# Stick-breaking attention: score tiles grouped otherwise, PSUM copies and sigmoids issued at other steps

## The chip, the cores and the metric

The kernel runs on one core of a Trainium2 chip. The metric is the device time of one execution in microseconds. TensorE (PE) does matrix products and transposes, VectorE (DVE) and ScalarE (ACT) do elementwise work and copies, GpSimd (POOL) does small fills, and SyncE (SP) issues most DMA transfers. Each engine works through its own queue in program order; semaphores hold an instruction until what it reads is there and what it overwrites is no longer read. Matmuls write PSUM, from which ACT or DVE copy to SBUF.

## What is computed

One layer of a decoder with batch 1 and 512 new tokens behind 16 meta tokens, and 8 running sequences of 4 tokens with 256 cached ones. The width is 1024. Two SwiGLU blocks enclose a mixer in which gated linear attention and stick-breaking attention run side by side. The change lies in the stick-breaking attention of 16 heads of 64, computed per pair of heads:

```python
def block(args):
    qblk, qi = args
    z = jnp.einsum('bqhd,bkhd->bhqk', qblk, k).astype(jnp.float32) * scale + bias_f
    mask = k_idx[None, :] < qi[:, None]
    l = jnp.where(mask, jax.nn.log_sigmoid(-z), 0.0)
    r = lax.cumsum(l, axis=3, reverse=True) - l
    a = jnp.where(mask, jnp.exp(jax.nn.log_sigmoid(z) + r), 0.0)
    return jnp.einsum('bhqk,bkhd->bqhd', a.astype(v.dtype), v)
```

The kernel takes the product of 1 - sigmoid(z) itself as a scan over the keys, from the right. It also returns the new key and value rows, of prompt and sample.

## The kernel before

**Main work.** Everything is computed in fp32 split into a high and a low part, with three products for one. The attention stage (about 587 to 806 us) projects queries, keys and values for eight pairs of heads. Its main work is a generator, `attention()`, that yields after each step of six matmuls. A pair has 8 steps for its queries (`tile_steps`, L728, L729, L731) and, from pair 1 on, 14 for keys and values together (`seven_steps`, L1079 to L1081: a 2 x 2 block product in seven products, from weight blocks b1, t, b2 and t4 and their sums). So pairs begin 22 steps apart (`BEGIN`).

`seven_steps` works in four PSUM accumulators a, d, b and c, and passes partial sums on: two steps after its start ACT copies a to b (L1069), at four d to a room (L1059), at six b to c (L1069 again) and b to a room (L1059), and so on. Each weight block is cast to its high part on ACT (L1006) and its low part is taken on DVE (L172). `weights_at` puts these at steps counted from the pair's start.

**Extra work.** What a pair needs beyond its projections is queued while the main work of the next pair runs. With n = `BEGIN[pr + 1]`, the list `pieces` puts each function at a step n + d: `scores` (three tiles n = 0, 1, 2 of the score matrix of both heads; L1996 on PE, then for each head e two sigmoids on ACT, L2001 and L2002, and POOL's fills), `scan` (L2015 on DVE), `weigh` (a product on DVE through the helper at L172, and the copy L2025), `rows_v` and `rows_k` (the new rows turned on PE, copied by ACT at L2046 and L2035, stored by SP), `tails` (L2053 to L2055 on PE, four DVE instructions from L2059 on), `turned` (the weights turned, L2078 on PE and L2081 on ACT, at the steps of `TURN`) with `meta_turned` at its end (L2104, L2105). `summed` and `meta_summed` multiply by the values, in the next pair's time. Pairs 4 to 7 also handle cached keys of the sample: `sample_keys` at n+14 (sixteen transposes L2181, four ACT copies L2183) and `sample_products` at n+16. Functions at one step are issued in the order in which they were listed; `later(k, f)` issues f some k steps on. A run of PE instructions between two main matmuls is called a group below.

**What sets the order.** The block runs in a manual schedule: each engine's queue is the order in which the Python code issues. `ps()` hands out four rotating PSUM buffers for extra work (pool `pp`, bufs=4). SBUF rooms come from an `Arena`, whose `take` reads the next place from the table `PLACES`; a room may only be written again when the instructions that used the place before are done, and so the table decides some waits.

Of the kernel before, what the change touches and what calls it, by code (L numbers as in the profile page):

```python
# [9 lines left out]
F32 = mybir.dt.float32  # L10
# [6 lines left out]
P = 128  # L17
# [3 lines left out]
NS = 32  # L21
# [41 lines left out]
3830686a0c606670241c46678584404844762f1b62261a50381e3c8c2c301036184c28722e3e427a683a6b604a0c08864e0966677040157b620e
2556201e58541a2f24352268843c3826443e34508c6a3b420c32604a6e0a0b7686082a09464e7a6284823a330e382e483c0006688c66704c0402
3e2c182514126a160a6e6072404a3043360d1c2a483b3c4208522e402c44464d3330100c504e0e424801362a10001c333c4d443206503140423e
0c3b040e023c4e081c0030482a363e0e023b4e1144060d0400403c104a524c4842461c0230362a0c3e40003c4a3d0608110400023a38484f524e
# [70 lines left out]
def hybrid_step(  # L137
# [2653 lines left out]
```

## Time and profile before

| | |
|---|---|
| timed runs | 1493.84, 1492.57 and 1585.64 us; median 1493.84 |
| profiled execution | 1492.2 us, its span 1490.5 us, granted TensorE clock 0.999 |
| busy, share of the span | PE 1477.0 us (99%), DVE 1085.3 (73%), ACT 804.9 (54%), POOL 57.0 (4%) |
| chain that ended last | PE 94%, DVE 3%, ACT 1%, DMA 1% |
| matmul instructions | 11905 |

The chain of work that ended last is followed back from the last instruction. In a row of the timeline stand the start, the duration, engine, line, operation, what is written and read, and how many instructions are taken together; in brackets stand the idle time of the engine ahead of it and the instruction that ended it. Matmuls overlap: each reads about 0.29 us, while the next starts 0.13 us later, so distances between starts say more than durations. L172 is a helper for all elementwise operations of two tensors, so its rows are told apart by their shapes.

### The profile page before, as it was taken

What the parts mean: (1) busy time and instruction counts of PE and PEld (TensorE: products, weight loads), DVE (VectorE), ACT (ScalarE), POOL (GpSimd) and SP (SyncE); (2) the same over time, 40 slices, a digit from 0 to 9 for tenths busy, and PEclk for the clock granted to TensorE, in tenths of its full rate; (3) what the DMA queues carried; (4) which work ended last, traced back from release to release, by engine and by line L of the source; (5) the groups of instructions that cost most, each with busy time, mean ns of one, the idle gap of its engine ahead of it and who ended that gap; (6) DMA issues with size and microseconds to landing.
All of it is one profiled execution on the core that took longest, in us unless ns stands there. A gap on an engine that the chain in (4) does not pass through costs nothing.

```text
span 1490.5 us, 29845 instructions
## 1 busy us (share of the span) xinstructions
PE 1477.0 (99%) x11905; PEld 1421.8 (95%) x11905; DVE 1085.3 (73%) x1820; ACT 804.9 (54%) x1513; POOL 57.0 (4%) x175
## 2 busy tenths in 40 slices
PE   9999999999999999999999999999999999999998
PEld 8999999999999898888988999999999999999998
DVE  5888888855677866887776754676567898888544
ACT  7455445533555656766775543644564455455334
POOL 2000000000000011201100000000000000000000
PEclk9999999999999999999999999999999999999999
DMA  8133333224665686567676866434531333333252
GB/s 253 50 93 100 100 91 103 85 79 130 170 147 132 164 160 175 108 115 139 141 122 181 246 143 198 97 103 147 156 112 51 100 100 101 98 106 93 79 174 93
DMA packets 288540, 187.60 MB, mean 126 GB/s; under 512 B 10988, under 2 KB 266674, under 8 KB 288402
## 3 DMA queue, kind: packets, MB, share of 16 engines
q1 hardware_dynamic: 280706, 181.97, 45.5%
q0 software_dynamic: 7680, 3.74, 2.5%
q8 instruction: 93, 1.52, 0.4%
q14 instruction: 45, 0.37, 0.1%
q10 hardware_dynamic: 16, 0.00, 0.0%
HBM read 160.63 MB, written 25.03 MB: 125 GB/s over the span
## 4 chain that ended last, share of the span: by engine, by line
PE 94%; DVE 3%; ACT 1%; DMA 1%; issue 0%; SPq 0%; DVEq 0%; ACTq 0%
PE acc L1300 8%; PE acc L1301 8%; PE acc L1302 8%; PE acc L741 6%; PE acc L744 6%; PE acc L742 6%; PE acc L728 5%; PE acc L729 5%; PE acc L731 5%; PE acc L1079 4%; PE acc L1081 4%; PE acc L1080 4%; PE acc L1242 2%; PE acc L1239 2%; PE acc L1240 2%; PE ps L1996 1%
## 5 line engine op out<-in xcount | busy, mean ns | idle before, releaser
L172 DVE TENSOR_TENSOR room<-room,room 128x560 fp32r<-128x560 f32 (+12 forms) x470 | 294.0, 645 | 84.2 <-ACT room L1059 17.0
L172 DVE TENSOR_TENSOR lo<-raw,hi 128x1024 fp32r<-128x1024 f32 (+1 forms) x207 | 248.1, 1199 | 80.3 <-ACT hi L1006 42.5
L1300 PE MATMUL acc<-room,hi 128*128 128x280 f32 (+1 forms) x896 | 259.9, 290 | 0.0
L1301 PE MATMUL acc<-room,hi 128*128 128x280 f32 (+1 forms) x896 | 259.7, 290 | 0.0
L1302 PE MATMUL acc<-room,lo 128*128 128x280 f32 (+1 forms) x896 | 259.5, 290 | 0.0
L1006 ACT CAST hi<-raw 128x1024 fp32r<-128x1024 f32 x114 | 119.7, 1054 | 142.8 <-PE acc L1301 49.2
L728 PE MATMUL acc<-room,hi 128*128 128x280 f32 x608 | 173.3, 302 | 0.6 <-DVE room L175 0.6
L1300 PEld LDWEIGHTS acc<-room,hi 128*128 128x128 f32 x896 | 168.8, 188 | 0.0
L1302 PEld LDWEIGHTS acc<-room,lo 128*128 128x128 f32 x896 | 168.6, 188 | 0.0
L1301 PEld LDWEIGHTS acc<-room,hi 128*128 128x128 f32 x896 | 168.5, 188 | 0.0
L729 PE MATMUL acc<-room,hi 128*128 128x280 f32 x608 | 163.7, 288 | 0.0
L1079 PE MATMUL acc<-room,hi 128*128 128x280 f32 x476 | 141.9, 298 | 2.1 <-ACT room L1059 1.1
L1081 PE MATMUL acc<-room,lo 128*128 128x280 f32 (+1 forms) x476 | 138.7, 291 | 1.3 <-DVE lo L172 1.3
L1080 PE MATMUL acc<-room,hi 128*128 128x280 f32 (+1 forms) x476 | 138.1, 290 | 0.0
L706 ACT CAST hi<-raw 128x1024 fp32r<-128x1024 f32 (+1 forms) x93 | 93.6, 1007 | 77.0 <-issue 21.6
L172 DVE TENSOR_TENSOR lo<-room,hi 128x1024 fp32r<-128x1024 f32 x106 | 101.1, 954 | 45.6 <-ACT hi L1006 45.4
L1006 ACT CAST hi<-room 128x1024 fp32r<-128x1024 f32 x106 | 88.9, 839 | 82.0 <-PE acc L1301 58.9
L731 PE MATMUL acc<-room,lo 128*128 128x280 f32 x608 | 125.7, 288 | 0.0
L728 PEld LDWEIGHTS acc<-room,hi 128*128 128x128 f32 x608 | 114.4, 188 | 6.8 <-issue 4.0
L729 PEld LDWEIGHTS acc<-room,hi 128*128 128x128 f32 x608 | 114.6, 188 | 0.3
L741 PE MATMUL acc<-room,hi 128*128 128x280 f32 (+2 forms) x388 | 110.7, 295 | 0.0
L742 PE MATMUL acc<-room,hi 128*128 128x280 f32 (+2 forms) x388 | 108.8, 290 | 0.0
(405 smaller groups left out, 3518.4 us busy)
## 6 DMA issues: line engine op xcount, KB each, us to landing
raw<-in_w_in_dram SPq DMA_DIRECT2D x68, 256.0 KB, 5.8
raw<-in_ffn_w_gate_dram SPq DMA_DIRECT2D x64, 256.0 KB, 3.1
raw<-in_ffn_w_up_dram SPq DMA_DIRECT2D x64, 256.0 KB, 3.4
raw<-in_ffn_w_down_dram SPq DMA_DIRECT2D x36, 448.0 KB, 3.8
raw<-in_w_in_dram SPq DMA_DIRECT2D x29, 512.0 KB, 7.4
out_dram<-room SPq DMA_DIRECT2D x36, 256.0 KB, 2.5
room<-in_cache_k_dram SPq DMA_DIRECT2D x32, 256.0 KB, 7.1
room<-in_cache_v_dram SPq DMA_DIRECT2D x32, 256.0 KB, 6.1
```

What stands on the lines that cost most here:

```text
L172: (eng or V).tensor_tensor(out=out, in0=a, in1=b, op=op)
L728: T.matmul(acc[h][:, :w], hi[k], act.get(k, h, w)[0], start=(k == order[0]), stop=False, skip_group_check=True)
L729: T.matmul(acc[h][:, : wid[h]], hi[k], a[h][1], start=False, stop=False, skip_group_check=True)
L731: T.matmul(acc[h][:, : wid[h]], lo[k], a[h][0], start=False, stop=(k == order[-1]), skip_group_check=True)
L741: T.matmul(acc[h][:nw, : wid[h]], wh, a[h][0], start=(k == 0), stop=False)
L742: T.matmul(acc[h][:nw, : wid[h]], wh, a[h][1], start=False, stop=False)
L1006: S.copy(hi[:, :kt], src)
L1079: T.matmul(x[:, :n], hi, act_[k][0][:, :n], start=(first and k == 0), stop=False, skip_group_check=True)
L1081: T.matmul(x[:, :w], lo, act_[k][0][:, :w], start=False, stop=(k == 3), skip_group_check=True)
L1300: T.matmul(x[:, :QW], hi, act[k][0], start=(first and k == 0), stop=False, skip_group_check=True)
L1301: T.matmul(x[:, :QW], hi, act[k][1], start=False, stop=False, skip_group_check=True)
L1302: T.matmul(x[:, :QW], lo, act[k][0], start=False, stop=(k == 3), skip_group_check=True)
```

## The change

Nothing is computed otherwise; PE, ACT, DVE, POOL and SP issue the same kinds of work in another order.

- `scores` 0 and 1 are both issued at n+3 (before at n+3 and n+6); `scores` 2 with `rows_v` and `rows_k` at n+11 (before `rows_v` at n+6, the others at n+10); `tails` at n+17 (before n+10), `turned` at n+17 and n+20 (before n+16 and n+19); `summed` two steps earlier. Scans and products on DVE move by up to one step.
- The copies of key and value rows, with their stores, come three and four steps after their transposes, those of the tails two steps after.
- The sigmoids of tile n and head e come `LAG[n][e]` steps after the matmuls.
- `PLACES` is replaced as a whole (cut below), and one room (`begun`) is given back five steps earlier at the end.

```diff
@@ -1879,6 +1879,7 @@
         return qz[pr // 2][:, 256 * (pr % 2) : 256 * (pr % 2) + 128 + more]
 
     own_ = slice(0, 64), slice(64, P)
+    LAG = (0, 1), (2, 4), (0, 2)
     AT, SCANS = (0, 416, 832), (slice(0, 416), slice(416, 816), slice(816, NW_))
 
     once = {}
@@ -1996,15 +1997,20 @@
                         T.matmul(p[e][:, c : c + k1 - k0], x[r, qc], y[r, kc], start=(x is qh and y is kh), stop=(x is ql))
                 c += k1 - k0
             d = slice(AT[n], AT[n] + c)
-            for e, (beta, keep) in enumerate(self.wide):
+
+            def weights(e):
+                beta, keep = self.wide[e]
                 hh = 2 * self.pr + e
-                S.activation(keep[:, d], p[e][:, :c], AF.Sigmoid, bias=sbb[:, 16 + hh : 17 + hh], scale=-1.0)
-                S.activation(beta[:, d], p[e][:, :c], AF.Sigmoid, bias=sbb[:, hh : hh + 1])
+                S.activation(keep[:, d], p[e][:, : d.stop - d.start], AF.Sigmoid, bias=sbb[:, 16 + hh : 17 + hh], scale=-1.0)
+                S.activation(beta[:, d], p[e][:, : d.stop - d.start], AF.Sigmoid, bias=sbb[:, hh : hh + 1])
                 for i, a, b in PARTS[1:]:
                     if d.start <= a < d.stop:
                         G.memset(keep[:, a : a + 1], 0.0)
                 if n == 2:
                     G.memset(beta[:, NW_ - 1 :], 0.0)
+
+            for e in range(2):
+                later(LAG[n][e], lambda e=e: weights(e))
             if n == 2:
                 give(*self.qs, *self.ks)
 
@@ -2031,21 +2037,29 @@
             p = ps()
             for j in range(4):
                 T.transpose(p[:, P * j : P * j + P], self.kf[:, NTL + P * j : NTL + P * j + P], ident)
-            kt = take(512)
-            S.copy(kt, p)
-            nc.sync.dma_start(kp_out[NM:, self.c0 : self.c0 + P].rearrange("(j p) f -> p j f", p=P),
-                              kt.rearrange("p (j f) -> p j f", f=P))
-            later(4, lambda: give(kt))
+
+            def out():
+                kt = take(512)
+                S.copy(kt, p)
+                nc.sync.dma_start(kp_out[NM:, self.c0 : self.c0 + P].rearrange("(j p) f -> p j f", p=P),
+                                  kt.rearrange("p (j f) -> p j f", f=P))
+                later(4, lambda: give(kt))
+
+            later(3, out)
 
         def rows_v(self):
 
             p = ps()
             for j in range(4):
                 T.transpose(p[:, P * j : P * j + P], self.vf[:, P * j : P * j + P], ident)
-            self.vt = vt = take(512)
-            S.copy(vt, p)
-            nc.sync.dma_start(vp_out[NM:, self.c0 : self.c0 + P].rearrange("(j p) f -> p j f", p=P),
-                              vt.rearrange("p (j f) -> p j f", f=P))
+
+            def out():
+                self.vt = vt = take(512)
+                S.copy(vt, p)
+                nc.sync.dma_start(vp_out[NM:, self.c0 : self.c0 + P].rearrange("(j p) f -> p j f", p=P),
+                                  vt.rearrange("p (j f) -> p j f", f=P))
+
+            later(4, out)
 
         def tails(self):
             pr, kf, vf = self.pr, self.kf, self.vf
@@ -2054,17 +2068,21 @@
             T.transpose(p[:NTL, P : 2 * P], vf[:, NP:], ident)
             T.transpose(p[:NR, 2 * P : 3 * P], vfm[pr % 2][:, :NR], ident)
             fc = slice(P * (pr % 4), P * (pr % 4) + P)
-            vm = once["vm"]
-            tk = take(P)
-            V.tensor_copy(tk[:NTL], p[:NTL, :P])
-            c = slice(self.c0, self.c0 + P)
-            nc.sync.dma_start(k_sample.rearrange("o b t h d -> (o b t) (h d)")[:, c], tk[:NS])
-            nc.sync.dma_start(kp_out[:NM, c], tk[NS:NTL])
-            later(LEAVE, lambda: give(tk))
-            V.tensor_copy(tail_v[pr // 4][:NTL, fc], p[:NTL, P : 2 * P])
-            V.tensor_copy(vm[:NR], p[:NR, 2 * P : 3 * P])
-            tt(vm[4 * NM : NR], p[4 * NM : NR, 2 * P : 3 * P], vm[4 * NM : NR].bitcast(F32), ALU.subtract)
             give(kf, vf)
+
+            def out():
+                vm = once["vm"]
+                tk = take(P)
+                V.tensor_copy(tk[:NTL], p[:NTL, :P])
+                c = slice(self.c0, self.c0 + P)
+                nc.sync.dma_start(k_sample.rearrange("o b t h d -> (o b t) (h d)")[:, c], tk[:NS])
+                nc.sync.dma_start(kp_out[:NM, c], tk[NS:NTL])
+                later(LEAVE, lambda: give(tk))
+                V.tensor_copy(tail_v[pr // 4][:NTL, fc], p[:NTL, P : 2 * P])
+                V.tensor_copy(vm[:NR], p[:NR, 2 * P : 3 * P])
+                tt(vm[4 * NM : NR], p[4 * NM : NR, 2 * P : 3 * P], vm[4 * NM : NR].bitcast(F32), ALU.subtract)
+
+            later(2, out)
 
         def turned(self, e, n):
 
@@ -2478,7 +2496,7 @@
 
     z, kT = take(512), {}
     E = mybir.EngineType
-    SK, SP, TURN = (14, 14, 14, 14), (16, 16), (16, 16, 16, 19, 19, 19)
+    SK, SP, TURN = (14, 14, 14, 14), (16, 16), (17, 17, 17, 20, 20, 20)
 
     TILE, PAIR, MIX0 = 8, 14, 24
     BEGIN = [0, 3 * TILE]
@@ -2544,7 +2562,7 @@
                 then(SUMS_BACK[i] + 6 + 4 * m, sums_hi, i, m)
                 then(SUMS_BACK[i] + 8 + 4 * m, sums_lo, i, m)
         for pr in range(8):
-            now, n, after = Pair(pr), BEGIN[pr + 1], BEGIN[pr + 2] if pr < 7 else BEGIN[8] + 18
+            now, n, after = Pair(pr), BEGIN[pr + 1], BEGIN[pr + 2] if pr < 7 else BEGIN[8] + 22
             if pr >= PLAIN:
                 weights_at(then, BEGIN[pr] + TILE, ("kv", pr), (-6, -6, -5, -4), t=(-3, -2), b2=(2, 3), t4=(5, 7))
                 then(BEGIN[pr] + 18, st.split, 1)
@@ -2552,15 +2570,15 @@
             if pr < 7:
                 then(BEGIN[pr] + 14, st.add)
                 then(BEGIN[pr] + 18, st.add)
-            pieces = [(3, now.scores, 0), (4, now.meta), (5, now.scan, 0, 0), (6, now.scan, 1, 0), (6, now.scores, 1), (6, now.rows_v),
-                      (8, now.scan, 0, 1), (9, now.weigh, 0, 0), (10, now.scan, 1, 1), (11, now.weigh, 1, 0),
-                      (10, now.scores, 2), (10, now.rows_k), (10, now.tails),
-                      (13, now.scan, 0, 2), (14, now.weigh, 0, 1), (15, now.scan, 1, 2), (16, now.weigh, 1, 1)]
+            pieces = [(3, now.scores, 0), (3, now.scores, 1), (4, now.meta), (6, now.scan, 0, 0), (7, now.scan, 1, 0),
+                      (8, now.scan, 0, 1), (9, now.weigh, 0, 0), (10, now.scan, 1, 1), (12, now.weigh, 1, 0),
+                      (11, now.scores, 2), (11, now.rows_v), (11, now.rows_k),
+                      (14, now.scan, 0, 2), (15, now.weigh, 0, 1), (16, now.scan, 1, 2), (17, now.weigh, 1, 1), (17, now.tails)]
             pieces += [(TURN[i], now.turned, i // 3, i % 3) for i in range(6)] + [(TURN[5], now.meta_turned)]
             for d, f, *args in pieces:
                 then(n + d, f, *args)
-            then(after + 3, now.summed)
-            then(after + 3, now.meta_summed)
+            then(after + 1, now.summed)
+            then(after + 1, now.meta_summed)
             if pr > 3:
                 for d, (q, b) in zip(SK, ((q, b) for q in range(2) for b in (pr - 4, pr))):
                     then(n + d, sample_keys, b, q, kps, kT)
@@ -2574,8 +2592,9 @@
         for d in (-14, -6, 2):
             when(d, ask)
         then(n + 18, lambda: todo.extend([n, f] for n, f in w0.pieces(1, 3)))
+        then(n + 18, lambda: give(once.pop("begun")))
         then(n + 21, lambda: give(*qz[:2]))
-        then(n + 23, lambda: give(*vfm, once.pop("begun"), *(once.pop(t) for t in ("az", "am", "vm"))))
+        then(n + 23, lambda: give(*vfm, *(once.pop(t) for t in ("az", "am", "vm"))))
         for n in range(1 - 2 * MIX0, 1):
             for f, args in mixer_at.pop(n, ()):
                 then(BEGIN[8] + MIX0 + n, f, *args)
```

Line numbers move: the scores are L1997 in the changed kernel, their sigmoids L2004 and L2005, the row copies L2043 (keys) and L2058 (values), the tails L2067 to L2069 on PE and from L2076 on DVE, the turned weights L2096 and L2099, the meta transposes L2122, the cached keys L2199 and L2201.

What stands in ACT's queue in the middle of pair 5 (n+10 to n+14), before. L2001 and L2002 are the sigmoids of tile 2, L2035 the copy of key rows, the first L1006 the high part of block b2 and the second that of t4, L1927 the high part of the next queries, L2183 the copies of cached keys:

```order
L2001 ACTIVATE room_104_5534<-ps_8628,sbb 128x512
L2002 ACTIVATE room_51_873<-ps_8628,sbb 128x512
L2001 ACTIVATE room_78_4589<-ps_8629,sbb 128x512
L2002 ACTIVATE room_129_8313<-ps_8629,sbb 128x512
L2035 COPY room_105_5554<-ps_8642 128x512
L1006 CAST hi_8659<-raw_8284 128x1024
L1059 COPY room_51_873<-acc_8597 128x280
L1006 CAST hi_8694<-room_70_4266 128x512
L1927 CAST room_75_4508<-room_99_5451 128x512
L1069 COPY acc_8599<-acc_8598 128x280
L1059 COPY room_99_5451<-acc_8598 128x280
L2183 COPY room_70_4266<-ps_8708 128x512
```

And after, where L2004 and L2005 are the sigmoids, L2043 is the copy of key rows and L2201 copies the cached keys:

```order
L1006 CAST hi_8618<-raw_8257 128x1024
L1059 COPY room_60_3148<-acc_8587 128x280
L2004 ACTIVATE room_76_4272<-ps_8631,sbb 128x512
L2005 ACTIVATE room_60_3148<-ps_8631,sbb 128x512
L2004 ACTIVATE room_103_5552<-ps_8632,sbb 128x512
L2005 ACTIVATE room_75_4271<-ps_8632,sbb 128x512
L1006 CAST hi_8675<-room_86_4753 128x512
L1928 CAST room_44_452<-room_104_5553 128x512
L1069 COPY acc_8589<-acc_8588 128x280
L1059 COPY room_103_5552<-acc_8588 128x280
L2043 COPY room_86_4753<-ps_8644 128x512
L2201 COPY room_128_8695<-ps_8690 128x512
```

The cast of b2 now stands ahead of the sigmoids of tile 2, and the copy of key rows behind L1069 and L1059, directly ahead of the copies of cached keys.

DVE's queue in pair 2, around the tails, before. L2059, L2064, L2065 and the L172 with 32x128 read the tails' PSUM buffer; lo is b2's low part:

```order
L2059 COPY room_105_5554<-ps_7550 48x128
L2064 COPY room_94_5300<-ps_7550 48x128
L2065 CAST room_123_6682<-ps_7550 96x128
L172 TENSOR_TENSOR room_123_6682<-ps_7550,room_123_6682 32x128
L1923 COPY room_94_5300<-room_99_5451 64x4x4 x4
L172 TENSOR_TENSOR room_78_4589<-room_78_4589,room_105_5554 128x815
L2025 COPY room_71_4267<-room_78_4589 128x6x16
L172 TENSOR_TENSOR lo_7561<-raw_7228,hi_7560 128x1024
L2015 SCALAR_TENSOR_TENSOR room_51_873<-room_51_873,room_77_4588 128x528
```

After, at the end of the pair's work; L2076, L2081, L2082 and the L172 behind them are the tails (the copy of 48 rows at L2076 is the first):

```order
L2021 SCALAR_TENSOR_TENSOR room_79_4590<-room_79_4590,room_74_4270 128x528
L172 TENSOR_TENSOR room_44_452<-room_76_4272,room_44_452 128x512
L172 TENSOR_TENSOR room_103_5552<-room_103_5552,room_79_4590 128x528
L2031 COPY room_95_5301<-room_103_5552 128x6x16
L172 TENSOR_TENSOR room_75_4271<-room_75_4271,room_79_4590 128x232
L172 TENSOR_TENSOR room_75_4271<-room_75_4271,room_79_4590 128x48
L2076 COPY room_76_4272<-ps_7618 48x128
L2081 COPY room_98_5485<-ps_7618 48x128
L2082 CAST room_40_340<-ps_7618 96x128
L172 TENSOR_TENSOR room_40_340<-ps_7618,room_40_340 32x128
```

The tails' four instructions have gone from ahead of b2's low part to behind the last product and the sums of the projection.

The start of pair 0's sigmoids on ACT, before, with what each waits for in brackets:

```order
L1006 CAST hi_6708<-raw_6191 128x1024 [waits DMASW1_49]
L2001 ACT_TABLE_LOAD [waits DVE_49]
L2001 ACTIVATE room_82_4675<-ps_6717,sbb 128x416 [waits PE_49]
L2002 ACTIVATE room_104_5534<-ps_6717,sbb 128x416 [waits DMAHW6_49,DMASW7_49]
L2001 ACTIVATE room_99_5451<-ps_6718,sbb 128x416 [waits DVE_49,PE_49,Activation_49]
L2002 ACTIVATE room_105_5554<-ps_6718,sbb 128x416 [waits DMAHW0_49]
```

And after:

```order
L1006 CAST hi_6705<-raw_6187 128x1024 [waits DMASW1_49]
L2004 ACT_TABLE_LOAD [waits DVE_49,PE_49]
L2004 ACTIVATE room_104_5553<-ps_6714,sbb 128x416 [waits Activation_49]
L2005 ACTIVATE room_103_5552<-ps_6714,sbb 128x416 [waits DMASW7_49]
L2004 ACTIVATE room_60_3148<-ps_6715,sbb 128x416 [waits DVE_49,DMAHW2_49,PE_49,Activation_49]
L2005 ACTIVATE room_79_4590<-ps_6715,sbb 128x416 [waits DMAHW7_49]
```

The load of the activation table (second row) waits for DVE before, and for DVE and PE after.

More of the change, by code (lines that the diff above doesn't have):

```diff
@@ L63 @@
[L63 to L66, printed above, removed]
-360e310c46441c103d2a304f0e4a483c364e0806424c460c103a0400021c432a2d480c4c40104f513e3c4930432a400e36424e4806080c3c1c38
@@ new lines @@
+341a1c18504c94707a2b6e7b467384442a90621e8048724e2228267664012450524d4b2e00446e7b2748492a1e20281f8584022c814e247b8044
+0052734a48456e842250471e266f81727a4e00012880444b84244a20466e451f484c6f007a1e8081722685202884046e4a486f441e8103727a00
+8020846e73024a2881204472046f461e6e4a024b2022031d827a847280606e788c6c3e7c5a5c364a8e74200368465e12888a0c444232667e301b
+342c542a2e4e192001244803261830291b34681e3a00331924010300691a04023368190124686900190403020112484e01682210211e5e2c8c06
+08902219262e842a665494338e0a425c56183a368826246e386a00100e0c6835287c805892018d55910b2d5d60435a8a343032463d458f852b95
@@ new lines @@
+076209675f2f3c7b707200746c407e761b1e200422781c62647a6810283e3d0c0e4100027b3c1b1a921c047a8a3c80004060583230347c1a166a
+14924c1c4e50824a4442483a12545c8c94188e04905a5e4653080a2a8567843230062e665d7d2c6a5294368850404e188c343e1c58007c8e2a03
+6032027a900a935a8a083c928567165c14804d042c6a4c486094067c2527363a52123288242a0a297a2e8e8a82908400506655544a1a16029203
+8f5a34603044464d2417426a386e9414067a2e3e7c482d0a2a2c8a1c8285678090844e6618508658928c2f295c384c3c5e56548e947a6e4a6a7c
+52483212028204008a6784882527062a37195c4e0b6a54363c48403e5e52182f5c2d2a1a567c1c3c254806372c185e50366a7c2b2d3e1c1a184e
@@ new lines @@
+0b2a404b3c4956545c5e252b06374e184856540b513e495c4b3c3653402c1c2e7c6a2a5e2537064e3e180b5456487c5c2e2a2c4b5e3a1c3c5336
+405138497c6a3e5c4e2506371c3c5356544818496a1a7c2a2e282c255c494b1a0b275e3a4e387c6a3640184e48062a361d54560b3e6a3c7c3a2c
+25402850522e3a3c270b3e085e067c6a4e5c48182a063a2756541d384e5e6a36287c50403c1a5c254e2f361848523e6a061c5e2a3748255c4e5e
+523e5c54561c066a080a7c3a40503c380a1c6a36252c2e1a180608154e6026134830124a3a4c7c508a38323c66181a2a600615405e3e085c6a7c
+17500a5a28121a263618244c1c1513068a5c5266063238243c504e4c3e8a281c085e5c0a295a28400614121c0626168a185a361a24383e3c401c
@@ new lines @@
+0e9092322c2a620c66361288223a74384f3c267056085a48644e6a7a5f30284958413e658a5c2b3234548c07530b2d3f6b4e084d6a7a4b3c8b5b
+4864414a062a2d550a8d5f4d522e7b5b6a8a5465504a41064e5a3e8b2c4c555c8c7b8a7a48566a5064540b6b5a583e075c417b7a5e2c8d4e488a
+068b6a526507540b413e7a5a645c8c8a8b064e5065086a493e077a54485d415c4e5e8c8a640a06086a7a420280846c1c487672885c661a743678
+7e120e1892908220224e10686e043c1e2a2e88482c545c5a92224e6620212c5e922a89881e2b5b935a2a2e88925f5a935e5b892a123c4e383a39
+923766885a524c36305e489066828e64
```

29 lines of the change are left out of this document (7 added, 22 removed).

## The prediction

> **What bounds the kernel now.** I read the page first: busy times, then the chain of waits.
>
> ```profile
> PE 1477.0 (99%) x11905; PEld 1421.8 (95%) x11905; DVE 1085.3 (73%) x1820; ACT 804.9 (54%) x1513; POOL 57.0 (4%) x175
> ...
> PE 94%; DVE 3%; ACT 1%; DMA 1%; issue 0%; SPq 0%; DVEq 0%; ACTq 0%
> ```
>
> TensorE is the bound over the whole span, and in 94% of the chain. The change removes no matmul, so it can win only PE's stalls and the price of breaking into the main stream. Next comes the view of waits for PE, in the attention stage (586 to 820 us):
>
> ```profile
> PE ps L2078 <- ACT room L2183: 1.7, 1, 1.7
> PE acc L1081 <- DVE lo L172: 1.3, 3, 0.4
> PE acc L1079 <- ACT room L1059: 0.7, 3, 0.3
> ```
>
> That is 3.7 us in seven places. All that can be won by removing waits is of this size. The view by windows shows pair 2, which has such waits, and pair 5, with more groups; its columns are window, sum, then PE, PE's weight loads, DVE, ACT and POOL:
>
> ```profile
> 643.60:671.80 28.20, 27.45 (x215) 24.21 (x214) 22.42 (x39) 19.13 (x37) 3.22 (x10) 1.00 0.62 111
> 729.60:759.20 29.60, 29.60 (x247) 26.35 (x246) 23.13 (x40) 21.09 (x41) 3.23 (x10) 1.00 0.71 140
> ```
>
> DVE is busy 22.4 of 28.2 us and ACT 19.1. They have room on average, so the question is in which order each does its queue. Busy time hides part of a stall (a waiting matmul reads longer), so I count below from start to start.
>
> **What is removed.** Pair 2, where the second weight block of the pair (b2, split into hi and lo) comes late. First PE, then ACT, then DVE:
>
> ```profile
> 656.27 0.29 PE L1081 MATMUL acc<-room,lo 128*128 128x280 f32 x1
> 656.83 0.40 PE L1079 MATMUL acc<-room,hi 128*128 128x280 f32 x1 [0.27 <-ACT room L1059]
> 657.06 0.29 PE L1080 MATMUL acc<-room,hi 128*128 128x280 f32 x1
> 657.80 0.40 PE L1081 MATMUL acc<-room,lo 128*128 128x280 f32 x1 [0.44 <-DVE lo L172]
> ...
> 654.94 0.60 ACT L2035 COPY room<-ps 128x512 f32<-128x512 f32 x1
> 655.40 1.08 ACT L1006 CAST hi<-raw 128x1024 fp32r<-128x1024 f32 x1
> ...
> 656.52 1.23 DVE L172 TENSOR_TENSOR lo<-raw,hi 128x1024 fp32r<-128x1024 f32 x1
> ```
>
> The price of breaking in comes from these rows (the third to fifth matmul of a group are left out):
>
> ```profile
> 651.35 0.29 PE L1081 MATMUL acc<-room,lo 128*128 128x280 f32 x1
> 651.57 0.50 PE L1996 MATMUL ps<-room,room 64*128 64x512 f32 x2
> ...
> 653.22 0.38 PE L1079 MATMUL acc<-room,hi 128*128 128x280 f32 x1
> 653.43 0.29 PE L1080 MATMUL acc<-room,hi 128*128 128x280 f32 x1
> 653.56 0.29 PE L1081 MATMUL acc<-room,lo 128*128 128x280 f32 x1
> ```
>
> Main matmuls start 0.13 us apart (653.43 to 653.56). Ahead of a group the step is 0.22, behind it 0.21: a group costs 0.09 + 0.08 = 0.17 us.
>
> The b2 stall is (0.56 - 0.13) + (0.74 - 0.13) = 1.04 us in pair 2, and the view of waits has three such pairs (0, 2 and 3; in 1 and 4 to 6 a cache group at step n+14 covers it): 3.1 us. The cause stands in the ACT rows: the cast of b2 waits its turn behind four sigmoids and a 0.60 us copy of key rows. After the change it stands ahead of those sigmoids, and the copy goes behind. On DVE the tails' copies and one product go from ahead of the lo part to behind it; below, with DVE's rows, stands why pairs 2 and 3 are then clear. I take all 3.1 as gone here and book what pair 0 keeps as an addition.
>
> Two smaller ones: the first turned group, and pair 7.
>
> ```profile
> 659.18 1.51 PE L2078 MATMUL ps<-ident,room 128*128 128x128 f32 x10
> 660.45 0.37 PE L1079 MATMUL acc<-room,hi 128*128 128x280 f32 x1
> ...
> 662.85 1.25 PE L2078 MATMUL ps<-ident,room 128*128 128x128 f32 x10
> 663.94 0.27 PE L2104 MATMUL ps<-ident,room 128*96 128x128 f32 x1
> ...
> 806.71 1.52 PE L2078 MATMUL ps<-ident,room 128*128 128x128 f32 x10 [1.72 <-ACT room L2183]
> ...
> 806.07 2.05 ACT L2183 COPY room<-ps 128x512 f32<-128x512 f32 x4 [3.77 <-DVE room L172]
> ```
>
> The same ten transposes take 1.27 us in the first turned group and 1.09 in the second: 0.2, and pair 0 is alike: 0.4. In pair 7, PE idles 1.72 us, and 0.29 - 0.13 more are covered by the last matmul's pipelined end: 1.9 us. ACT's copies of turned cache keys wait 3.77 us, because their destination is a room that a late DVE product still reads. The new table of places gives them rooms that wait for no such product; this 1.9 goes. Removed in all: 3.1 + 0.4 + 1.9 = 5.4 us.
>
> **What is added.** *Groups.* Counted in the order of instructions, pairs 0 to 3 have five groups before and five after (the key and value rows join the third score tile, but the old sums become a group of their own, and the tails move into the first turned group). Pairs 4 to 7 have six before and seven after, since the sample's products at step n+16 no longer meet the turned group, which moves to n+17. Over the program main is broken into 163 times before and 165 after: 2 x 0.17 = +0.3.
>
> *Pairs 4 to 6, a PSUM buffer held.* There are four buffers. At n+14 sixteen transposes of cache keys take all four in turn. The rows before, around that place in pair 5, PE and then ACT:
>
> ```profile
> 742.38 1.91 PE L2181 MATMUL ps<-ident,room 128*128 128x128 f32 x16
> 744.04 0.38 PE L1079 MATMUL acc<-room,hi 128*128 128x280 f32 x1
> ...
> 743.65 0.44 ACT L1069 COPY acc<-acc 128x280 f32<-128x280 f32 x1
> 743.98 0.44 ACT L1059 COPY room<-acc 128x280 f32<-128x280 f32 x1
> 744.26 2.10 ACT L2183 COPY room<-ps 128x512 f32<-128x512 f32 x4
> ...
> 651.74 0.38 ACT L1069 COPY acc<-acc 128x280 f32<-128x280 f32 x1 [0.52 <-PE acc L1081]
> ```
>
> Here the sixteen run at 1.66 / 16 = 0.10 us each, unhindered. After the change the key rows' buffer is still full: its copy, which was done by then, is given at n+14 and stands on ACT behind two casts and the copies L1069 and L1059. L1069 can't start until the last matmul of step n+13 is done; 651.74 against that matmul's start at 651.35 gives 0.39 us. On the clock of these rows that start is 742.25, so L1069 at 742.64, L1059 0.33 later at 742.97, the row copy 0.28 later at 743.25, done 0.60 after that at 743.85. PE would start the third tile at 742.38 + 8 x 0.10 = 743.2. The hold is 0.65 us, if ACT is free by then; if ACT is as late as before (L1069 at 743.65), it is 1.65. ACT's queue starts one step of six matmuls later (0.78), but without the row copy (0.46 from start to start), b2's cast (0.95) and a copy of 0.28 ahead: 743.65 + 0.78 - 1.69 = 742.7. So I take 0.65: three pairs, 1.95; bounds 1.5 (the row copy done after 0.46) and 5.0. Nothing at all is excluded, since L1069 can't come before its matmul. In pair 7 no L1069 stands there: nothing.
>
> *Pairs 1 to 3, the tails.* Their copies now come at n+19, last in DVE's queue, and the meta transposes at n+20 want their PSUM buffer.
>
> ```profile
> 646.12 0.62 ACT L2002 ACTIVATE room<-ps,sbb 128x416 f32<-128x416 f32 x1
> 646.60 1.06 ACT L1006 CAST hi<-room 128x1024 fp32r<-128x1024 f32 x1
> ...
> 647.70 1.22 DVE L172 TENSOR_TENSOR lo<-room,hi 128x1024 fp32r<-128x1024 f32 x1 [0.25 <-ACT hi L1006]
> ...
> 653.50 0.28 DVE L2059 COPY room<-ps 48x128 f32<-48x128 f32 x1 [1.41 <-PE ps L2055]
> ...
> 663.51 0.52 DVE L172 TENSOR_TENSOR room<-room 128x232 f32<-128x232 f32 x2
> 663.94 1.23 DVE L172 TENSOR_TENSOR lo<-raw,hi 128x1024 fp32r<-128x1024 f32 x1
> ```
>
> Before, DVE goes from the lo part at 647.70 to 663.94 in 16.2 us, 1.4 of it idle for the tails: 14.8 us of work. After, the cast ahead of that lo part stands behind two sigmoids more (0.48 each by 646.12 to 646.60, +1.0), one scan of about 1.0 comes behind the lo part instead of ahead, and the tails are at the end of the same work: 647.70 + 1.0 + 14.8 + 1.0 = 664.5. (For b2 the same count gives: 656.52 - 647.70 = 8.8, less 1.4 of idle, 1.0 of tails (653.50 on, four rows) and 1.0 of product, plus 1.0 of scan, is 6.4; its lo part starts at 647.70 + 1.0 + 6.4 = 655.1 and is done at 656.3, and PE wants it at 657.06 + 0.13 - 0.43 = 656.8.) PE reached its meta transposes at 663.94; one step later and without 1.04 of stall that is 663.7. So up to 0.8 us of the b2 gain is paid back here. Bounds 0 (another buffer free in time, DVE idle elsewhere shorter) and 1.2; over three pairs I take 0.6 each, +1.8.
>
> *Pair 0, the table load.*
>
> ```profile
> 585.68 1.06 ACT L1006 CAST hi<-raw 128x1024 fp32r<-128x1024 f32 x1
> 586.76 1.28 ACT L2001 ACT_TABLE_LOAD   x1
> 588.40 0.61 ACT L2001 ACTIVATE room<-ps,sbb 128x416 f32<-128x416 f32 x1 [0.35 <-PE ps L1996]
> ```
>
> Before, the load of the sigmoid's table waits for DVE alone and is over before the first scores are. After, the load itself carries the wait for the scores: sigmoids start 1.28 us later, and the queues behind them with it. Against the 0.5 us that b2 has to spare by the count above that is 0.8 to 0.9 late, so most of pair 0's 1.04 stays. The tails (up to 0.9, as above) and the first turned group (up to 0.5) come on top: 2.3 at most, 1.1 if these two are mostly absorbed; I take 1.7. The page "ScalarE: Activation LUTs" of the Trainium skill (section What ACT_TABLE_LOAD costs) has a drain of about 1.38 us beside a load of 1283 ns, 2.66 in all; by that the term would be about 1.4 more. The trace agrees on the load and shows no drain ahead of it (the cast from 585.68 ends where the load starts), so the sum goes without.
>
> *Queues.* The moved copies take their stores along, three and four steps later for the rows, two and more for the tails. SP issues in order, so a store that waits for its copy holds weight loads behind it, for about as long as the holds above, under a step. Now no wait of PE in the view of waits ends at a DMA, and the DMA engines are at 0.62 to 0.71 in the windows: nothing, and a microsecond a pair if a load has no such reserve. POOL's small fills go with the sigmoids that they follow, and POOL is busy 3.2 us of 28: nothing.
>
> Sum: -5.4 + 0.3 + 1.95 + 1.8 + 1.7 = +0.35. On the profiled run's 1492.2 us (span 1490.5 and 1.7 around it) that is 1492.6; the lower two of the three timed runs, 1492.57 and 1493.84, lie 1.0 above it on average, of which I add 0.4: **1493.0**.
>
> **Rivals.** *A, the forecast:* stalls go, new ones of like size come; 1491 to 1496. Chance 0.50.
>
> *B, the new holds mostly don't appear.* For it: ACT and DVE idle some 9 and 6 us of each 28, and a few tenths earlier on ACT make each hold vanish. Against: the matmul ahead of L1069. With the lower bounds, -5.4 + 0.3 + 1.5 + 0 + 1.1 = -2.5, with pair 0 free too -3.6: 1489.0 to 1490.1 with the 0.4, and 1487 to 1491 with the runs' scatter. 0.28.
>
> *C, slower: the PSUM hold governs.* Place: the third and fourth cache tile at n+14 of pairs 4 to 6. It decides from the point where a hold exceeds (5.4 - 0.3 - 1.8 - 1.7) / 3 = 0.53 us; with ACT as late as before, 1.65 each, the tails at 1.2 and pair 0 at 2.3: -5.4 + 0.3 + 5.0 + 3.6 + 2.3 = +5.8: 1498.4 with the 0.4. For it: four buffers, all taken by one group. The Trainium skill's "Perfetto Trace Analysis" (Optimization Strategy) reads a gap that repeats on the engine that should be saturated as a sign of too little SBUF or PSUM for the next tile. Before the change no run here shows such a gap at these transposes (1.66 us for sixteen). Against: ACT is 0.95 us earlier. 0.16.
>
> *D, it does what its words say*, two groups fewer in each of eight pairs: 16 x 0.17 = 2.7 us, with the stalls gone and no holds 1492.2 - 5.4 - 2.7 = 1484.1, 1484.5 with the 0.4. The count of groups speaks against it. 0.04. Something unseen, 0.02.
>
> **Numbers.** The likeliest is A. The range 1487 to 1498 holds A and B and a third of C; D, the rest of C and the unseen are left out, some 0.17. Beyond 2% (30 us, about what a measurement of this kernel can tell from no change) no case reaches: faster 0.01, same 0.97, slower 0.02 for a new dependence that the order doesn't price.
>
> **What would show it.** Right: no wait of L1079 or L1081 behind b2 in pairs 2 and 3, some in pair 0; no 1.7 us wait in pair 7; PE waiting at the third cache tile (L2199 of the changed kernel) in pairs 4 to 6 for ACT's row copy (L2043 there), 0.5 to 0.8 each; PE waiting at the meta transposes (L2122 there) for DVE in pairs 0 to 3; the first sigmoid about 1.3 us after the scores. Wrong: no wait at the cache tiles (B), or one over 1.2 us (C); windows of pairs 4 to 6 that are shorter than 29.6.

## The result and the profile after

The changed kernel takes 1500.63 us (median of five, 1498.65 to 1501.31) against 1493.66 for the kernel before: 1.0049 times as long, 95% interval 1.0033 to 1.0065. One of the five runs before took 1585.64 us, in a slower state; the ratio leaves it out. The forecast was 1493.0, with a range up to 1498.0: it is slower by 7 us, where no change was forecast, and the range misses it. The time lies where rival C put it (1498.4) and beyond.

The page of the changed kernel, busy times and chain:

```profile
PE 1477.6 (99%) x11905; PEld 1423.7 (95%) x11905; DVE 1081.4 (72%) x1820; ACT 804.8 (54%) x1513; POOL 59.0 (4%) x175
...
PE 90%; DVE 3%; ACT 2%; DMA 2%; issue 1%; SPq 1%; DVEq 0%; ACTq 0%
```

The same work, 6.4 us more of span (1496.9). The profiled run is the fastest of the five (1498.65 us). PE waits in the attention stage, 586 to 826 us of the changed kernel:

```profile
PE ps L2199 <- ACT room L2043: 4.4, 3, 1.5
PE acc L1079 <- ACT acc L1069: 2.1, 2, 1.0
PE ps L2199 <- ACT room L2005: 1.5, 3, 0.5
PE acc L1081 <- DVE lo L172: 0.8, 1, 0.8
PE ps L2122 <- DVE room L172: 0.6, 1, 0.6
PE ps L2178 <- ACT room L2005: 0.2, 1, 0.2
```

Of the old waits none is left but one at b2's low part, in pair 0. The six lines are 9.6 us, 8.8 of them new; the first and third belong to the cache tiles of pairs 4 to 6. The windows from one pair's first query matmul to the next show where the time is. First the kernel before, pairs 3 to 6, then the changed one:

```profile
666.73:694.87 28.14, 27.44 (x217) 24.22 (x216) 22.38 (x40) 19.14 (x37) 3.26 (x10) 1.00 0.90 120
694.87:724.49 29.62, 29.62 (x248) 26.34 (x247) 23.07 (x41) 20.98 (x41) 3.20 (x10) 1.00 0.62 156
724.49:754.16 29.67, 29.67 (x249) 26.39 (x247) 23.14 (x41) 21.09 (x41) 3.23 (x10) 1.00 0.74 164
754.16:783.81 29.65, 29.65 (x248) 26.36 (x247) 22.97 (x41) 21.17 (x41) 0.66 (x8) 1.00 0.62 102
```

```profile
666.80:694.45 27.65, 26.61 (x216) 24.14 (x215) 21.80 (x40) 19.15 (x37) 3.26 (x10) 1.00 0.90 157
694.45:726.55 32.10, 30.03 (x248) 26.32 (x247) 22.52 (x41) 21.07 (x41) 3.23 (x10) 1.00 0.52 132
726.55:758.62 32.07, 30.00 (x248) 26.29 (x247) 22.43 (x41) 21.07 (x41) 3.23 (x10) 1.00 0.62 134
758.62:792.25 33.63, 31.56 (x249) 27.93 (x247) 22.55 (x41) 21.26 (x41) 0.71 (x8) 0.95 0.58 112
```

Pair 3 gained 0.5 us, pairs 4, 5 and 6 lost 2.5, 2.4 and 4.0; pair 6 has a granted clock (the column of 1.00) of 0.95. The 8.9 us lost there are more than the whole result; pairs 2, 3 and 7 gained some (0.6, 0.5 and 2.4). The cause shows on ACT and PE in pair 5 (the first two rows of L2199 stand for four transposes each, the third for the next six):

```profile
739.28 1.05 ACT L1006 CAST hi<-raw 128x1024 fp32r<-128x1024 f32 x1
742.40 0.39 ACT L1059 COPY room<-acc 128x280 f32<-128x280 f32 x1 [2.06 <-PE acc L1081]
742.68 0.69 ACT L2004 ACTIVATE room<-ps,sbb 128x512 f32<-128x512 f32 x1
...
746.00 0.43 ACT L1069 COPY acc<-acc 128x280 f32<-128x280 f32 x1
746.32 0.43 ACT L1059 COPY room<-acc 128x280 f32<-128x280 f32 x1
746.61 0.63 ACT L2043 COPY room<-ps 128x512 f32<-128x512 f32 x1
...
744.01 0.66 PE L2199 MATMUL ps<-ident,room 128*128 128x128 f32 x4
745.16 0.66 PE L2199 MATMUL ps<-ident,room 128*128 128x128 f32 x4 [0.50 <-ACT room L2005]
747.29 0.93 PE L2199 MATMUL ps<-ident,room 128*128 128x128 f32 x6 [1.47 <-ACT room L2043]
```

The four sigmoids of tile 2 have their scores from about 740.5 on, but ACT stands 2.06 us idle ahead of L1059: that copy waits for a matmul of step n+11, and it is ahead of the sigmoids in ACT's queue. The order quoted in the section on the change shows it there, too. A lag of 0 in `LAG` doesn't mean at once: `later` runs a function at the next step at the earliest, and at n+12 the copy of the projection, queued when the pair's values began, comes first. So ACT reaches L1069 at 746.00, and the copy of key rows behind it at 746.61, while PE has been at the cache tiles since 744.01.

### The profile page after: what moved, and what is told of

It is laid out like the page before. It is cut to its first block, busy times and chain, and to the rows that moved or that the text cites. A ratio compares the mean times of both kernels' runs of the same rounds, so it can differ in the third digit from the quotient of the medians.

```text
span 1496.9 us, 29837 instructions
## 1 busy us (share of the span) xinstructions
PE 1477.6 (99%) x11905; PEld 1423.7 (95%) x11905; DVE 1081.4 (72%) x1820; ACT 804.8 (54%) x1513; POOL 59.0 (4%) x175
## 4 chain that ended last, share of the span: by engine, by line
PE 90%; DVE 3%; ACT 2%; DMA 2%; issue 1%; SPq 1%; DVEq 0%; ACTq 0%
PE acc L1300 8%; PE acc L1302 8%; PE acc L1301 8%; PE acc L741 6%; PE acc L742 6%; PE acc L744 6%; PE acc L728 5%; PE acc L729 4%; PE acc L731 4%; PE acc L1079 4%; PE acc L1081 3%; PE acc L1080 3%; DVE room L172 1%; PE acc L1242 1%; PE acc L1239 1%; PE acc L1240 1%
## 5 line engine op out<-in xcount | busy, mean ns | idle before, releaser
L172 DVE TENSOR_TENSOR room<-room,room 128x280 f32<-128x280 f32 (+13 forms) x462 | 288.2, 643 | 84.0 <-ACT room L808 18.3
L172 DVE TENSOR_TENSOR lo<-raw,hi 128x1024 fp32r<-128x1024 f32 (+1 forms) x207 | 248.1, 1199 | 98.0 <-ACT hi L1006 60.3
L1006 ACT CAST hi<-raw 128x1024 fp32r<-128x1024 f32 x114 | 119.6, 1053 | 141.5 <-PE acc L1301 49.5
L172 DVE TENSOR_TENSOR lo<-room,hi 128x1024 fp32r<-128x1024 f32 x106 | 101.3, 955 | 56.5 <-ACT hi L1006 56.3
L1006 ACT CAST hi<-room 128x1024 fp32r<-128x1024 f32 x106 | 88.9, 839 | 82.3 <-PE acc L1301 60.1
```

Of the source, the lines that this page charges most:

```text
L172: (eng or V).tensor_tensor(out=out, in0=a, in1=b, op=op)
L1006: S.copy(hi[:, :kt], src)
```

## The experiments

Two theories were set against each other. Q: the sigmoids behind L1059 make ACT late, and all else follows. P: the key rows' PSUM buffer, given back at n+14, is what holds PE. The ratios are to the kernel before, run beside each; its own median moved by 1.4 us from one set of runs to another, so differences below go by the ratios where they are small. In rows_early, rows_both, best_a, best_b, best_c and the two kernels of groups the table `PLACES` differs too, since rooms are taken at other times (45 of its 1508 places in rows_early, 90 in rows_both).

| kernel | median us | ratio, 95% interval |
|---|---|---|
| the change | 1500.63 | 1.0049 (1.0033 to 1.0065) |
| s2_inline: tile 2's sigmoids at once | 1493.86 | 1.0008 (0.9999 to 1.0018) |
| rows_early: key rows' copy at once | 1499.68 | 1.0044 (1.0027 to 1.0061) |
| rows_both: both row copies at once | 1493.51 | 1.0005 (0.9996 to 1.0015) |
| before_lag: the kernel before, tile 2's sigmoids late | 1493.02 | 1.0003 (0.9994 to 1.0013) |
| table: the table loaded early | 1498.10 | 1.0039 (1.0025 to 1.0053) |
| turn16: first turned group of pairs 0 to 3 at n+16 | 1500.53 | 1.0049 (1.0034 to 1.0065) |
| best_a: sigmoids, both row copies, table | 1490.03 | 0.9982 (0.9973 to 0.9991) |
| best_b: and the queries' split later | 1486.84 | 0.9961 (0.9947 to 0.9974) |
| best_c: and the row copies behind L1059 | 1485.89 | 0.9954 (0.9940 to 0.9967) |
| groups: best_b, products in the turned group | 1513.32 | 1.0139 (1.0124 to 1.0155) |
| groups_b: the same with other places | 1487.65 | 0.9964 (0.9951 to 0.9978) |

**The sigmoids at once.**

```diff
             for e in range(2):
-                later(LAG[n][e], lambda e=e: weights(e))
+                if n == 2:
+                    weights(e)
+                else:
+                    later(LAG[n][e], lambda e=e: weights(e))
```

> The changed kernel, but the sigmoids of score tile 2 are issued with its matmuls at n+11, not a step and two steps later; tiles 0 and 1 keep their lags. Theory Q (ACT's queue: a copy of the projection, L1059, which waits for matmuls of step n+11, stands ahead of these sigmoids and idles ACT for 2.06 us): the sigmoids start 2.0 us earlier; PE's wait for L1069 in pairs 2 and 3 goes (2.4 us), the hold at the cache tiles falls from 2.4 to about 0.8 us in each of pairs 4 to 6 (4.8), so about 7.2 us less than the changed kernel, near 1493.4. Rival P (PSUM: the key rows' buffer is given back at n+14, whatever stands ahead): the waits for the row copy stay at 1.5 each, only the 2.4 goes, near 1498.2.

Measured 1493.86, 6.8 us less by the medians and 6.1 by the ratios, where Q expected 7.2 and P 2.4. PE's waits, s2_inline:

```profile
PE ps L2202 <- ACT room L2046: 3.6, 4, 1.3
PE ps L2125 <- DVE room L172: 2.1, 4, 0.6
PE acc L1081 <- DVE lo L172: 0.8, 1, 0.8
PE ps L2099 <- DVE room L172: 0.2, 1, 0.2
```

L2202 and L2046 are here the cache tiles and the key rows' copy: three waits of 0.77 in pairs 4 to 6, where each had 2.0, and one of 1.3 us in pair 7, which had none. L1069 is gone. What came out in its place is the wait of the meta transposes for the tails, 2.1 us in four pairs (L2125): with PE no longer stopped ahead of it, DVE's chain is the next thing late.

**One row copy at once.** In `rows_k`:

```diff
-            later(3, out)
+            out()
```

> The changed kernel, but the copy of the key rows and its store come at n+11, right behind their transposes, so that their PSUM buffer is empty long before the cache tiles. Rival P: the wait at the third cache tile goes and nothing else is late: 4.4 us less, near 1496.2. Theory Q: that wait moves to the fourth tile, which needs ACT's first copy of a cache tile, and the second tile keeps waiting for the sigmoids: the hold falls from 2.4 to about 2.0 in each pair, 1.4 us less in all, near 1499.2; the waits for L1069 in pairs 2 and 3 stay at 1.0 each.

Measured 1499.68, 0.7 us less by the ratios and not to be told from the change by the intervals; P expected 4.4 less and Q 1.4. P as put is out: the hold moved to the fourth tile, which waits for ACT's first copy of a cache tile. The first two lines of the view:

```profile
PE ps L2199 <- ACT room L2201: 4.4, 3, 1.5
PE ps L2199 <- ACT room L2005: 2.3, 5, 0.7
```

**One part of the change alone.** In the kernel before, with its loop over the heads made a function `weights(e)`:

```diff
-            for e, (beta, keep) in enumerate(self.wide):
+            for e in range(2):
+                if n == 2:
+                    later(2, lambda e=e: weights(e))
+                else:
+                    weights(e)
```

> The kernel before, with one part of the change alone: the sigmoids of tile 2 are issued two steps after their matmuls, at n+12, and so behind L1059. Theory Q: they start about 2.8 us later; L1069 is done about 1.1 us late for its reader at n+16 in pairs 0, 2 and 3, the second cache tile waits about 1 us for its PSUM buffer in pairs 4 to 6, while some 0.7 of the 1.04 at b2 goes: 4 to 5 us slower than before, near 1498. Rival P (the late row copies are the cause, and these stay early here): no slower than before, 1 to 2 us faster by the waits at b2.

Q expected 4 to 5 us more; it is 0.8 by the medians, and the interval holds 1. P expected 1 to 2 less. So the place of the sigmoids alone isn't the cause either. It isn't free: pairs 4 to 6 take 30.15 to 30.18 us each, 0.5 more than before, though no line below belongs to them; pairs 0 to 3 gain 0.6 in all and pair 7 gains 0.4. PE's waits, before_lag:

```profile
PE acc L1081 <- DVE lo L172: 2.0, 3, 0.7
PE ps L2085 <- ACT room L2190: 1.3, 1, 1.3
```

No cache tile of pairs 4 to 6 waits in this view, and there is no L1069 (the 1.3 is in pair 7): here the row buffers are empty by n+14, so the tiles take those first and the sigmoids' buffers last. Hence a third theory: a hold needs both, late sigmoids and late row copies, since the four tiles take the buffers in the order in which the code gives them back; either half cures it.

**Both row copies at once**, the sigmoids still late. In `rows_k` and `rows_v`:

```diff
-            later(3, out)
+            out()
...
-            later(4, out)
+            out()
```

> The changed kernel with both row copies, key and value, and their stores at n+11, right behind their transposes; the late sigmoids stay. The cache tiles then take the two row buffers first, and the sigmoids are done by the time of the third and fourth. If the hold comes from row copies and sigmoids together (either one early cures it), the waits at the cache tiles go to under 0.3 us a pair and with them the stretch at half clock: 7.5 to 9 us less than the changed kernel, 1491.5 to 1493; the waits for L1069 in pairs 2 and 3 stay at 1.0 each. If the late sigmoids alone made it (theory Q as first put), PE waits for them at the fourth tile, 1 to 2 us a pair, and the time stays over 1495.

Measured 1493.51: 7.1 us less by the medians, 6.6 by the ratios, somewhat short of the 7.5 to 9 expected, with 1.0 in each of pairs 2 and 3 for L1069 still there and not one wait at the cache tiles of pairs 4 to 6 (the 0.8 is pair 7's):

```profile
PE acc L1079 <- ACT acc L1069: 2.1, 2, 1.0
PE acc L1081 <- DVE lo L172: 0.8, 1, 0.8
PE ps L2122 <- DVE room L172: 0.8, 2, 0.6
PE ps L2199 <- ACT room L2005: 0.8, 2, 0.5
```

But part of the hold went where the view of waits doesn't show it. The sixteen products of the sample behind the cache tiles (L2213) take 2.01 us from their start to the next main matmul in each of pairs 4 to 6, and 1.00 in the changed kernel. First rows_both, then the changed kernel, pair 5:

```profile
746.05 2.08 PE L2213 MATMUL ps<-room,room 128*32 128x256 f32 x16
...
745.36 2.09 ACT L2201 COPY room<-ps 128x512 f32<-128x512 f32 x4
```

```profile
749.91 1.07 PE L2213 MATMUL ps<-room,room 128*32 128x256 f32 x16
```

In rows_both ACT is still copying the cache tiles when the products begin, and they start in four batches 0.47 to 0.49 us apart, each as a copy ends. As matmuls overlap, PE reads as busy throughout. So the cure is a partial one: pair 4 takes 30.48 us, against 32.10 in the changed kernel and 29.62 before.

**The wait for L1069.** In before_lag the same copy was about as late (658.17, and 658.60 in the changed kernel), and nobody waited. There the turned group stands at n+16, right ahead of L1069's reader; the change moved it to n+17.

```diff
-            pieces += [(TURN[i], now.turned, i // 3, i % 3) for i in range(6)] + [(TURN[5], now.meta_turned)]
+            pieces += [(TURN[i] - (pr < 4 and i < 3), now.turned, i // 3, i % 3) for i in range(6)] + [(TURN[5], now.meta_turned)]
```

> The changed kernel with the first turned group of pairs 0 to 3 back at n+16 (the tails stay at n+17 and so become a group of their own). If PE waits for L1069 in pairs 2 and 3 only because the turned group no longer stands ahead of its reader at n+16, those waits (1.04 each, 2.4 us with what follows them) go; the group's third tile then waits about 0.7 us for DVE's product in each pair, and four groups more cost 4 x 0.17 = 0.7: between 1.5 us less than the changed kernel and no change. If the cover isn't the point, the waits for L1069 stay.

The waits for L1069 are gone, so the group was their cover. The time is the same: the third turned tile now waits for DVE's product, 1.0 to 1.3 us in pairs 0, 2 and 3, not 0.7 (one line of the view):

```profile
PE ps L2096 <- DVE room L172: 3.4, 3, 1.3
```

**The table load.** Ahead of pair 0's scores, on a tile of one column:

```diff
                 self.wide = [(take(NW_), take(NW_)) for _ in range(2)]
+                if self.pr == 0:
+                    warm = cp.tile([P, 1], F32, tag="warm", name="warm")
+                    S.activation(warm, sbb[:, :1], AF.Sigmoid)
```

> The changed kernel with one added sigmoid of a single column that depends on nothing, issued just ahead of pair 0's scores, so that the activation table is loaded before the scores are there. If the load behind the wait causes pair 0's two waits (0.97 us at b2's lo part, 0.74 at the meta transposes), the first sigmoid starts 1.28 us earlier and both waits go: 1.7 us less, near 1498.9. If DVE's order keeps them in part: 0.7 us less.

ACT at the start of pair 0, first the changed kernel, then table:

```profile
588.44 1.28 ACT L2004 ACT_TABLE_LOAD   x1 [1.69 <-issue]
589.73 0.61 ACT L2004 ACTIVATE room<-ps,sbb 128x416 f32<-128x416 f32 x1
```

```profile
586.25 1.28 ACT L1993 ACT_TABLE_LOAD   x1
587.54 0.20 ACT L1993 ACTIVATE warm<-sbb 128x1 f32<-128x1 f32 x1
587.93 0.61 ACT L2007 ACTIVATE room<-ps,sbb 128x416 f32<-128x416 f32 x1 [0.18 <-ACT warm L1993]
```

In table the scores start 0.52 us earlier (586.87, not 587.39), so of the 1.80 between the first sigmoids 1.28 are the load, as expected. Both of pair 0's waits (b2, tails) went, too. In their place pair 0 has the wait for L1069 that pairs 2 and 3 have, now three times 1.0 us:

```profile
PE acc L1079 <- ACT acc L1069: 3.1, 3, 1.0
```

Measured is about 1.5 us less (ratio 1.0039 against 1.0049), close to the 1.7, but the intervals overlap, and the trace has a new wait of 1.0 against the two that went.

**All repairs together.** best_a joins the edits of s2_inline, rows_both and table, with places for the rooms that are taken earlier.

> The changed kernel with three repairs: sigmoids of tile 2 at n+11, both row copies at n+11, the activation table loaded ahead of pair 0's scores. No hold at the cache tiles, no wait for L1069, none at b2; the tails' wait at n+20 (0.3 to 0.6 us in pairs 0 to 3 once the others are gone) remains. About 5.4 gained on the kernel before, less 0.3 for two groups and 2.1 for the tails: 1489 to 1490.5.

Measured 1490.03, as expected. The waits left are DVE's tails (1.3 us) and 0.4 to 0.5 at L1059, which now stands behind the row copies. PE issues the same order in the changed kernel, s2_inline, rows_both and best_a, so pair 4 shows what each half does: 29.72 us with neither late (best_a), 30.48 with late sigmoids alone (rows_both), 30.36 with late row copies alone (s2_inline), 32.10 with both. Each alone costs 0.6 to 0.8, and together they cost 2.4, more than their sum: the third theory holds, but either repair leaves a part.

best_b adds, in `queries`:

```diff
-            for n, f in ((3, samples), (6, hi), (9, lo)):
+            for n, f in ((3, samples), (10, hi), (13, lo)):
```

> As best_a, and the split of the next pair's queries into high and low part (L1928 on ACT, 0.52 us, and a difference of 0.67 us on DVE) four steps later, so that DVE reaches the tails 0.67 us earlier. The tails' waits (0.3 to 0.6) go: 1.5 to 2 us less than best_a, 1487 to 1489.

Measured 1486.84, 3.2 us less than best_a, more than the 1.5 to 2 expected; the tails' waits are gone, which by starts in the traces is 1.8. Another 1.3 comes from the sample's products in pairs 4 to 6: 1.42 us each in best_a, 1.00 here, where the split no longer stands ahead of the copies of cache tiles in ACT's queue. PE's waits, best_b:

```profile
PE acc L1079 <- ACT room L1059: 1.3, 3, 0.5
PE ps L2102 <- DVE room L172: 0.2, 1, 0.2
```

best_c puts both row copies behind L1059:

```diff
-            out()
+            later(1, out)
```

> As best_b, with both row copies one step later (n+12), behind L1059 instead of ahead of it. The waits for L1059 in pairs 0, 2 and 3 (0.43 each) go: 1.3 us less than best_b, near 1485.5. If the cache tiles then miss the row buffers again, 0 to 0.5 us a pair more in pairs 4 to 6.

Measured 1485.89, 1.0 us less by the medians, where 1.3 was expected; the intervals overlap. The waits for L1059 are gone, 1.1 us at the meta transposes came back, and pair 7 has 0.3 for the copy of value rows. The gain isn't at L1059: by starts, best_c is 0.24 us ahead when pair 4 begins, 0.16 of it from ahead of pair 0, and 0.8 more comes in pair 7, where the sample's products take 1.00 us and not 1.96. This is the lowest median of the study, 0.9954 of the time before (0.9940 to 0.9967).

**The groups.** best_b with the products one step later, and a new table of places, since rooms are taken at other times:

```diff
-    SK, SP, TURN = (14, 14, 14, 14), (16, 16), (17, 17, 17, 20, 20, 20)
+    SK, SP, TURN = (14, 14, 14, 14), (17, 17), (17, 17, 17, 20, 20, 20)
```

> As best_b, with the sample's products at n+17 in the turned group, so that pairs 4 to 7 have six groups and not seven. By 0.17 us a group 0.7 us less than best_b. If the fifth PSUM buffer of that group isn't free in time (the products then wait for ACT's first turned copy), 0 to 0.5 us a pair more.

Measured 1513.32, 26 us more. The table of places is to blame, not the groups: ACT waits 9.21 us to write a room that a store of rows still reads, and two more such waits are 7.9 (ACT) and 7.4 us (DVE). From SP's queue and ACT's, groups, pair 3:

```profile
682.41 0.49 SPq L2050 DMA_DIRECT2D out_dram<-room  x1
...
695.51 0.62 ACT L1928 CAST room<-room 128x512 fp32r<-128x512 f32 x1 [9.21 <-DMA out_dram<-room]
```

So it was run again with best_b's table but for eight places:

> As best_b, with the sample's products at n+17 in the turned group, and best_b's table of places but for eight entries, so that no room is taken right behind a store that still reads it. Six groups in pairs 4 to 7 and not seven: by 0.17 us a group 0.7 us less than best_b, near 1486.1; up to 0.5 us a pair more where the fifth PSUM buffer comes late.

Measured 1487.65, 0.8 us more than best_b and not 0.7 less; the intervals overlap. Most of the 0.8 is in pair 4 (29.91 us against 29.34), where the scores wait 0.3 us for a product of DVE. The windows of pair 5, best_b and then groups_b, are level:

```profile
720.77:750.05 29.28, 29.28 (x248) 26.45 (x247) 22.47 (x41) 20.86 (x41) 3.25 (x10) 1.00 0.73 161
```

```profile
721.38:750.74 29.36, 29.34 (x249) 26.35 (x248) 22.68 (x41) 21.08 (x41) 3.27 (x10) 1.00 0.71 160
```

A group fewer gave nothing: with five tiles in one group the last waits for a PSUM buffer (0.27 us in pair 7). Whether the saved 0.17 is wholly eaten in the other pairs too was not taken apart.

## Why the prediction was wrong

- **What is removed** was right. b2's waits are gone in pairs 2 and 3, the small one at pair 2's turned group too, and pair 7's 1.7 us. What pair 0 keeps was right in kind and size: 0.82 at b2 and 0.60 at the tails by the view of waits, 0.97 and 0.74 from start to start, 1.7 in all as booked.
- **The PSUM hold** is the step that failed. The third tile does wait for the row copy, but the hold was booked at 0.65 us a pair and is 2.48 (32.10 less 29.62). What the booking left out is that the sigmoids' buffers come late as well: the second tile waits 0.50 for them, and ACT does the row copy only behind them. With the sigmoids at once (s2_inline) the row copy holds PE for 0.77, near the 0.65. The false term is the time at which ACT reaches L1069: "ACT's queue starts one step of six matmuls later (0.78)". I moved the old rows by a step and took away what had left the queue. I did not ask what the first instruction of the new queue waits for: L1059, ahead of the sigmoids, has to wait for a later matmul than they do, and cost 2.06 us. The bound for ACT "as late as before", 1.65, was no bound for this reason; it is exceeded by 0.8.
- **Rival C** named the place rightly, the holds are past its point of decision (0.53 us), and it had 0.16. Its price stopped short because of the same bound, and for the clock below.
- **L1069's own reader** was left out altogether. The copy was costed only as something ahead of the row copy, while its reader at n+16 lost its cover, the turned group, by the change: 2.4 us in pairs 2 and 3.
- **The tails** in pairs 1 to 3 were booked at 1.8 us and cost nothing there: in pairs 2 and 3 PE was already late by the wait for L1069, and pair 1 has 0.2 at another wait for ACT (L2178). They came out in s2_inline, at 0.3 to 0.6 a pair, about as booked. So the term was right as a next limit and wrong as a sum: terms on different engines were added, though PE pays only for the latest.
- **The groups** were counted rightly (no two fewer a pair), and their price of 0.17 us could not be collected by merging one (groups_b).
- **The table's drain**: the trace has the first sigmoid 0.01 us behind the 1.28 us load, so leaving a drain out of the sum was right. The Trainium skill, "ScalarE: Activation LUTs" (What ACT_TABLE_LOAD costs), has 1.38 us for it, which no run here shows.

Sum by the measured terms: -5.4 as removed, +7.4 for three holds (2.48, 2.40 and, without the clock, 2.5), +1.5 for the clock, +2.4 for L1069, +1.7 for pair 0, +0.2 in pair 1, +0.3 for groups: +8.1 against 6.4 in span. The terms of pairs 2 and 3 are too high by about 0.5 each, as their windows show (27.65 against 28.14 in pair 3), and pair 7 gained 2.4, not 1.9 (from its start to the next query matmul 72.61 us, 74.97 before). That leaves about 0.2.

## What to carry to other kernels

When an instruction is moved to another step, look at the instruction that will stand directly ahead of it in its engine's queue and at what that one waits for; shifting the old timeline by a step misses a wait that wasn't there before. Where a group takes all buffers of a pool, the order in which they are given back decides who is waited for, so ask which two are last, not only which one. And stalls on several engines don't add up: repairing one bares the next (here L1069, then the tails, then L1059), so a repair is judged by what PE waits for afterwards. The view of waits is not enough for that where matmuls overlap: compare starts too, since 1 us a pair at the sample's products read as busy time.

## What was not expected of the hardware

**PE's clock can halve behind two waits in one group of transposes.** In pair 6 of the changed kernel:

```profile
777.24 0.66 PE L2199 MATMUL ps<-ident,room 128*128 128x128 f32 x4 [0.50 <-ACT room L2005]
779.36 1.93 PE L2199 MATMUL ps<-ident,room 128*128 128x128 f32 x8 [1.47 <-ACT room L2043]
780.94 0.58 PE L1079 MATMUL acc<-room,hi 128*128 128x280 f32 x1
781.32 0.43 PE L1080 MATMUL acc<-room,hi 128*128 128x280 f32 x1
781.55 0.43 PE L1081 MATMUL acc<-room,lo 128*128 128x280 f32 x1
...
779.30:782.90 3.60, 3.54 (x16) 3.54 (x17) 0.36 (x1) 2.64 (x6) 0.00 (x0) 0.53 0.20 65
```

From the end of the second wait on the last eight transposes start 0.21 us apart instead of 0.11, and main matmuls 0.23 instead of 0.13, for some 3.5 us in all (the last row is a window, granted clock 0.53). The pair is 1.5 us longer than pairs 4 and 5 (33.63 against 32.10), whose waits are the same to a hundredth. In rows_early, table and turn16, which have such waits (0.38 to 0.50 and 1.46 to 1.47), two of the three pairs show it; in s2_inline and rows_both none. So 7 of 12 such groups slowed the clock; what decides which is open. That fits the spread of the timed runs: 2.7 us for the changed kernel, 0.7 for rows_both. A single wait of 1.72 us, pair 7 before the change, did nothing of the kind. The Trainium skill, "TensorE: Matmul & The Clock Gate" (Why this matters for your kernels), warns of idle gaps over about 3 us; here two gaps of 0.50 and 1.47 us sufficed, with only transposes around them, for 5.2 us from the last main matmul to the next (775.69 to 780.94). The same page of the Trainium skill (Part 4: PE-mode transpose) says that transposes don't count as busy in the same way, which would agree; no run here separates the two.

**A place can cost more than an order.** The kernels groups and groups_b differ in the table of places alone, in 87 of its 1508 entries, and by 26 us; the store whose room was wanted at once had been issued 13 us before it let go (682.41 to 695.51).
